# Expert top-k scores copied out of PSUM by ScalarE, and more buffers for the gathered expert rows, in a two-layer diffusion backbone step

## Chip, cores and metric

The kernel runs on one core of a Trainium2 chip. The metric is the device time of one execution in microseconds; a kernel's time is the median of its runs. Engines are named as the profile names them: PE is TensorE (PEld its weight loads), DVE is VectorE, ACT is ScalarE, POOL is GpSimd, SP is SyncE, which here only issues DMAs.

## What is computed

A prompt of 128 tokens and a sample of 512 tokens go through two layers, each a token mixer (attention and gated linear attention, GLA) and a product-key expert mixer (PEER). Prompt and sample meet only in the weights. The change lies in the expert mixer, which is computed for blocks of 128 tokens:

```python
def one_block(xt):                                   # 128 tokens x 1024
    q = (xt @ wq).reshape(128, 8, 2, 128)            # 8 heads, 2 halves
    s = jnp.einsum('thpd,pnd->thpn', q, sub_keys)    # 128 scores for each half
    s1, i1 = lax.top_k(s[:, :, 0], 16)
    s2, i2 = lax.top_k(s[:, :, 1], 16)
    cand = (s1[..., :, None] + s2[..., None, :]).reshape(128, 8, 256)
    sc, ci = lax.top_k(cand, 16)
    idx = ...                                        # 16 experts of 16384, per head
    g = jax.nn.softmax(sc, axis=-1)
    a = jax.nn.gelu(jnp.einsum('td,thkd->thk', xt, u[idx]))
    return jnp.einsum('thk,thkd->td', g * a, v[idx])
```

So each token needs 128 rows of u and 128 rows of v, 4 KB each, chosen by its own top-k.

## The kernel before

**Blocks.** The prompt is one block, the sample four. The prompt's block and two of the sample's (`ROWS`, blocks 0 and 1) fetch the chosen expert rows: one indirect DMA issued by POOL brings, for one of the 128 slots, one row of 4 KB for each of the 128 tokens (512 KB, `gather`, L887). For u, DVE multiplies the fetched tile with the token's activations and sums along the row (`u_rows`, L904); for v, DVE adds the weighted tile to an accumulator (`v_rows`, L934). Below, a **u row** or **v row** is one such slot: a gather of 512 KB and one DVE instruction. The other two sample blocks (`DENSE`, blocks 2 and 3) go the dense way: PE multiplies with all 16384 experts. Their u is streamed in 128 tiles of 512 KB (`uc`, matmuls `hp`), ACT applies the gelu into `Q`, DVE writes for groups of 16 tokens a one-hot selection (`spread`: `A` L1042, `eq` L1047, `bw` L1050), PE turns it into gates (`Gp`, L1057), DVE multiplies `Q` by them (L1062), and PE multiplies with v, streamed in 128 tiles `v` (`vacc`, L1083). The 128 experts of a half key are cut into four chunks of 32 (`CIS`), each with 16 groups of tokens: below, chunk 3 group 2 means the third group of the last chunk. `A`, `eq` and `bw` have two buffers each, so DVE can be two groups ahead of PE.

**Top-k.** `front` makes the indices. For each head PE writes the two sets of 128 scores into a PSUM tile `sc` (L812), and `top16` (L784 to L789) lets DVE search them: MAX8, FIND_INDEX8, MATCH_REPLACE8 read the scores in PSUM, then MAX8 and FIND_INDEX8 read the rest in an SBUF tile `wk`. For the sample, `sc` shares two PSUM buffers (`psm`, tag mm1) with `hp` and `Gp`.

**Buffers.** Gathered tiles live in a ring of `gat` buffers: `PB` = 6 for the prompt, `GB` = 6 for the sample in both layers. The ring also takes the residual rows and three vectors that finish a block (`load_x1`, `load_fin`), which SP loads.

**Order.** Tracks of work are woven by hand-written shares (`weave`), and a scheduler then sorts each engine's instructions by a simulated timeline. Each engine's queue is therefore fixed when the program is built, and the engine takes it in that order. SP issues all direct DMAs in one queue: a load that waits for its buffer holds up the loads behind it.

**Stages**, by the profile: sample mixer of layer 0 beside the prompt's mixer and gathers (to about 1520 us), sample experts of layer 0 beside the prompt's mixer of layer 1 (to 3100), sample mixer of layer 1 beside the prompt's gathers (to 4170), sample experts of layer 1 (to the end). In the experts' stages the gathers go u rows of block 0, v rows of block 0, u rows of block 1, v rows of block 1.

Of the kernel before, what the change touches and what calls it, by code (L numbers as in the profile page):

```python
# [7 lines left out]
F32 = mybir.dt.float32  # L8
# [3 lines left out]
AF = mybir.ActivationFunctionType  # L12
# [13 lines left out]
NK = 128  # L26
# [5 lines left out]
CW = 256  # L32
UC = 256
SB = 4
PB = 6
UBS = (4, 4)
HG = 4
LEAD = (1, 1, 2, 2, 2)
# [11 lines left out]
AB = 12  # L50
QBS = (3, 4)
TG = 16
GB = 6
U0 = 56
YB = 3
PAIRS = [(i, j) for i in range(TOPK) for j in range(TOPK) if (i + 1) * (j + 1) <= TOPK]
# [7 lines left out]
def kernel(ctx: ExitStack, tc, xp, xs, ck, cv, st, cond, adaw, adab, win, wglr,  # L64
                              nrm, w2, gb, gn, wao, wgo, wout, lnp, wq, sk, pu, put, pv, rope, cst, msk,
                              yp, ys, nk_out, nv_out, ns_out):
    nc = tc.nc

    def sided(tr):
        side = ("right", "left")[tr]  # L70
        return lambda name: tc.tile_pool(name=name + str(tr), bufs=1, side=side, reuse_waits="tile")

    def opener(stack, tr):
        mk = sided(tr)
        return lambda name: stack.enter_context(mk(name))
# [15 lines left out]
    def psm(name, tr=0):  # L91
        return ps.tile([128, 512], F32, tag=f"mm{tr}", bufs=2, name=name)
# [690 lines left out]
    def top16(v, i, src, n):  # L783
        nc.vector.max(v[:, 0:8], src)  # L784
        nc.vector.max_index(i[:, 0:8], v[:, 0:8], src)
        wk = sm.tile([128, NK], F32, tag="wk", bufs=2, name="wk")
        nc.vector.match_replace(wk[:, 0:n], v[:, 0:8], src, -3.0e38)  # L787
        nc.vector.max(v[:, 8:16], wk[:, 0:n])
        nc.vector.max_index(i[:, 8:16], v[:, 8:16], wk[:, 0:n])  # L789

    def front(tr, l, b, res, own, groups, near):
# [5 lines left out]
        for n in groups:  # L797
            tv = own.tile([128, HG, 2, TOPK], F32, tag=f"tv{tr}", bufs=2 - tr, name="tv")
            ti = own.tile([128, HG, 2, TOPK], U32, tag=f"ti{tr}", bufs=2 - tr, name="ti")
            for h in range(n):  # L800
                hh = h0 + h
                assert lp[l]["qp", tr] > hh
                if near:
                    qs = [lp[l]["q", tr, 2 * hh + k][:, b * 128:(b + 1) * 128] for k in range(2)]
                else:
                    qT = sm.tile([128, 2, 128], F32, tag="qT", bufs=CB, name="qT")
                    nc.sync.dma_start(qT, tops[tr, l][2 * hh:2 * hh + 2, :, b * 128:(b + 1) * 128]
                                      .rearrange("k p t -> p k t"))
                    qs = [qT[:, k, :] for k in range(2)]
                s = psm("sc", tr)  # L810
                for k in range(2):
                    nc.tensor.matmul(s[:, k * NK:(k + 1) * NK], qs[k], lp[l]["sk"][:, k, :], start=True, stop=True)  # L812
                for k in range(2):
                    top16(tv[:, h, k, :], ti[:, h, k, :], s[:, k * NK:(k + 1) * NK], NK)
                yield 2
# [288 lines left out]
    def weave(*tracks):  # L1104
        live = [[t[0][2], list(t)] for t in tracks]
        while live:
            e = min(live, key=lambda v: v[0])
            g, total, a, b = e[1][0]
            try:
                v = next(g)  # L1110
                e[0] += v * (b - a) / total
                yield v
            except StopIteration:
                e[1].pop(0)
                if e[1]:
                    e[0] = max(e[0], e[1][0][2])
                else:
                    live.remove(e)
# [10 lines left out]
    def take(g, n):  # L1129
        for _ in range(n):  # L1130
            yield next(g)
# [11 lines left out]
    def s_peer(l):  # L1143
        ms, m = parts[l]
        with ExitStack() as st_:
            assert parts["p_peer", l] == "done"
            parts["p_close", l].close()
            p = Peer(1, l, opener(st_, 0)("sgat"), GB)
            r0, r1 = ROWS
            d0, d1 = DENSE  # L1150
            f0, u0 = p.front(r0, LEAD, True), p.u_rows(r0)

            def lead():
                for n in LEAD:
                    yield from take(m, n)
                    yield from take(f0, 3 * n + 1)
                for _ in m:
                    pass

            yield from weave([(lead(), 160.0, 0.0, 1.0)], [(take(u0, U0), 1.5 * U0, UP, 1.0)])  # L1160
            for _ in f0:
                pass
            ms.close()
            parts["s_peer", l] = "open"
            ds = ExitStack()
            p.up = opener(ds, 1)("dense")
            r, f = RF, FF
            yield from weave([(p.dense(p.up, DENSE), 1010.0, DF[0], DF[1])],
                             [(u0, 192.0 - 1.5 * U0, r[0], r[1]), (p.v_rows(r0), 197.0, r[1], r[2]),
                              (p.u_rows(r1), 192.0, r[2], r[3]), (p.v_rows(r1), 197.0, r[3], r[4])],  # L1170
                             [(p.front(d0), 50.0, 0.0, f[0]), (p.front(d1), 50.0, f[0], f[1]),
                              (p.front(r1), 50.0, f[2], f[3])])
        fs = parts["fin"] = ExitStack()
        fp = opener(fs, 0)("fin")
        ds.close()
        yield from p.settle(fp, DENSE)
        if l == L - 1:
            fs.close()
# [22 lines left out]
    def p_front(l):  # L1201
        peers[l] = Peer(0, l, None, PB)
        yield from peers[l].front(0)
# [111 lines left out]
```

## Time and profile before

| | |
|---|---|
| median of 3 runs | 5521.72 us (5514.61 to 5526.49) |
| profiled execution | 5526.76 us |
| its span, first to last instruction | 5525.0 us |
| PE busy | 4570.1 us (83%) |
| DVE busy | 3905.2 us (71%) |
| POOL busy | 2251.5 us (41%) |
| ACT busy | 1041.1 us (19%) |
| mean granted PE clock | 0.894 |

Two engines are busy for most of the time, PE and DVE, and neither all the time: they take turns in being the one that the others wait for. The table of shares hides that; it has to be read stage by stage.

### The profile page before, as it was taken

What the parts mean: (1) busy time and instruction counts of PE and PEld (TensorE: products, weight loads), DVE (VectorE), ACT (ScalarE), POOL (GpSimd) and SP (SyncE); (2) the same over time, 40 slices, a digit from 0 to 9 for tenths busy, and PEclk for the clock granted to TensorE, in tenths of its full rate; (3) what the DMA queues carried; (4) which work ended last, traced back from release to release, by engine and by line L of the source; (5) the groups of instructions that cost most, each with busy time, mean ns of one, the idle gap of its engine ahead of it and who ended that gap; (6) DMA issues with size and microseconds to landing.
All of it is one profiled execution on the core that took longest, in us unless ns stands there. A gap on an engine that the chain in (4) does not pass through costs nothing.

```text
span 5525.0 us, 71758 instructions
## 1 busy us (share of the span) xinstructions
PE 4570.1 (83%) x26668; PEld 3388.7 (61%) x26668; DVE 3905.2 (71%) x8024; ACT 1041.1 (19%) x1860; POOL 2251.5 (41%) x1652
## 2 busy tenths in 40 slices
PE   8879988877776789799999668689877458998998
PEld 5658665655655566467774445578776347675743
DVE  4342368887499996967656798864248999978682
ACT  4231123322211201010000222145221010000000
POOL 0000017675355552343441476620135656245450
PEclk9979998988887799899999778788988679998999
DMA  5325558998388888799996688830447889698995
GB/s 180 117 69 176 190 183 320 318 327 304 135 311 322 326 310 314 249 352 342 369 364 236 215 305 290 300 112 19 133 135 258 323 313 356 214 397 302 409 331 204
DMA packets 472735, 1440.71 MB, mean 261 GB/s; under 512 B 55232, under 2 KB 123968, under 8 KB 472384
## 3 DMA queue, kind: packets, MB, share of 16 engines
q0 software_dynamic: 221184, 805.40, 39.9%
q1 hardware_dynamic: 251200, 630.71, 32.4%
q8 instruction: 209, 3.42, 0.2%
q14 instruction: 142, 1.16, 0.1%
HBM read 1391.29 MB, written 44.63 MB: 260 GB/s over the span
## 4 chain that ended last, share of the span: by engine, by line
DVE 16%; PE 16%; issue 8%; DMA 7%; POOL 2%; ACT 1%; another core or an unknown queue 1%; SPq 0%; DVEq 0%; POOLq 0%; ACTq 0%
DMA gat<-in_pv,idx 4%; PE vacc L1083 4%; DVE gat L904 4%; PE gt L151 3%; DVE acc L934 3%; DMA gat<-in_pu,idx 2%; PE proj L151 2%; PE po L151 2%; POOL gat L887 1%; PE hp L151 1%; DVE A L1042 1%; PE qp L151 1%; DVE Q L1062 1%; DVE bw L1050 1%; PE pTp L626 1%
## 5 line engine op out<-in xcount | busy, mean ns | idle before, releaser
L887 POOL DMA_INDIRECT gat<-in_pu,idx x768 | 991.9, 1292 | 886.8 <-DVE gat L904 382.2
L887 POOL DMA_INDIRECT gat<-in_pv,idx x768 | 962.7, 1253 | 789.4 <-DVE acc L934 468.0
L934 DVE SCALAR_TENSOR_TENSOR acc<-gat,dots,acc 128x1024 f32<-128x1024 f32 x762 | 999.0, 1311 | 155.8 <-DMA gat<-in_pv,idx 141.4
L904 DVE SCALAR_TENSOR_TENSOR gat<-gat,h 128x1024 f32<-128x1024 f32 x768 | 945.1, 1242 | 141.4 <-DMA gat<-in_pu,idx 129.8
L151 PE MATMUL hp<-h2Td,uc 128*128 128x256 f32 x4096 | 947.9, 392 | 76.3 <-DVE wk L787 48.9
L1083 PE MATMUL vacc<-v,Q 128*128 128x512 f32 x2048 | 925.2, 605 | 14.3 <-DMA v<-in_pv 13.6
L151 PEld LDWEIGHTS hp<-h2Td,uc 128*128 128x128 f32 x4096 | 799.3, 197 | 199.7 <-DVE wk L787 52.2
L136 POOL TENSOR_TENSOR wl<-w,wh 128x1024 fp32r<-128x1024 f32 x92 | 232.0, 2521 | 1447.2 <-ACT wh L134 1358.1
L1083 PEld LDWEIGHTS vacc<-v,Q 128*128 128x128 f32 x2048 | 384.7, 193 | 456.5 <-issue 437.0
L134 ACT ACTIVATE wh<-w 128x1024 fp32r<-128x1024 f32 x184 | 194.2, 1057 | 706.4 <-PE proj L151 282.7
L996 ACT ACTIVATE Q<-hp 128x512 f32<-128x512 f32 x128 | 76.4, 597 | 1117.0 <-PE hp L151 1022.7
L151 PE MATMUL proj<-wh,hTh 128*128 128x256 f32 x896 | 264.1, 295 | 7.2 <-DVE sgo L486 3.4
L151 PE MATMUL proj<-wl,hTh 128*128 128x256 f32 x896 | 262.0, 292 | 5.5 <-POOL wl L136 5.5
L151 PE MATMUL proj<-wh,hTl 128*128 128x256 f32 x896 | 263.7, 294 | 0.0
L1057 PEld LDWEIGHTS <-A 128*128 128x128 bf16 x6144 | 174.6, 96 | 132.5 <-issue 61.7
L136 DVE TENSOR_TENSOR wl<-w,wh 128x1024 fp32r<-128x1024 f32 x92 | 127.8, 1389 | 173.6 <-ACT wh L134 163.4
L1057 PE MATMUL Gp<-bw,A 128*128 128x32 bf16 x6144 | 181.0, 177 | 77.4 <-DVE bw L1050 57.3
L151 PE MATMUL po<-V,pT 128*128 128x64 f32 x1600 | 220.0, 279 | 10.2 <-ACT pT L628 8.4
L151 PEld LDWEIGHTS po<-V,pT 128*128 128x128 f32 x1600 | 211.1, 201 | 20.0 <-ACT pT L628 12.7
L151 PE MATMUL modr<-w,csil 128*2 128x256 f32 x768 | 193.9, 405 | 21.4 <-DMA w<-in_adaw 17.7
L618 DVE TENSOR_REDUCE nm<-s 128x1 f32<-128x768 f32 (+1 forms) x160 | 130.9, 819 | 114.0 <-PE s L151 112.7
L151 PEld LDWEIGHTS proj<-wh,hTh 128*128 128x128 f32 x896 | 176.1, 197 | 18.1 <-issue 13.2
(297 smaller groups left out, 7567.1 us busy)
## 6 DMA issues: line engine op xcount, KB each, us to landing
uc<-in_put SPq DMA_DIRECT2D x256, 512.0 KB
v<-in_pv SPq DMA_DIRECT2D x256, 512.0 KB
w<-in_win SPq DMA_DIRECT2D x208, 512.0 KB
w<-in_adaw SPq DMA_DIRECT2D x96, 512.0 KB
w<-in_wq SPq DMA_DIRECT2D x64, 512.0 KB
w<-in_wgo SPq DMA_DIRECT2D x32, 512.0 KB
w<-in_wao SPq DMA_DIRECT2D x32, 512.0 KB
w<-in_wout SPq DMA_DIRECT2D x32, 512.0 KB
```

The source lines that it names most:

```text
L134: nc.scalar.activation(wh, r, AF.Copy)
L136: (nc.vector, nc.gpsimd)[i].tensor_sub(wl, r, f32(wh))
L151: nc.tensor.matmul(out, lt, rt, start=(i == 0), stop=(i == n - 1))
L618: nc.vector.tensor_reduce(nm, s[:, 0:KEYS], axis=AX.X, op=OP.max, negate=True)
L626: nc.tensor.transpose(t[:, (kc - c0) * 128:(kc - c0 + 1) * 128], pr[:, kc * 128:(kc + 1) * 128], ident)
L887: i = nc.gpsimd.indirect_dma_start(out=t, out_offset=None, in_=src, in_offset=bass.IndirectOffsetOnAxis(ap=self.res[b][0][:, k:k + 1], axi ...
L904: nc.vector.scalar_tensor_tensor(u, u, 1.0, h2, op0=OP.mult, op1=OP.mult, accum_out=dots[:, k:k + 1])
L934: nc.vector.scalar_tensor_tensor(acc, v, w_, acc, op0=OP.mult, op1=OP.add)
L996: nc.scalar.activation(q[:, i:i + 2, :].rearrange("p i t -> p (i t)"), t, AF.Gelu_apprx_tanh)
L1042: nc.vector.tensor_tensor(a.rearrange("p t (i w) -> p t i w", w=2), pairs[:, None].to_broadcast([128, TG, NK // 2, 2]), i1[:, sl, None, :] ...
L1057: nc.tensor.matmul(t[:, j * CI:(j + 1) * CI], a[:, j, :], bw[:, j, q, :], start=(q == 0), stop=(q == 2))
L1083: nc.tensor.matmul(accs[i][:, s * 512:(s + 1) * 512], w[:, j, i * 128:(i + 1) * 128], v[:, s * 512:(s + 1) * 512], start=(key == 0), stop= ...
```

## The change

```diff
-PB = 6
+PB = 8
-GB = 6
+GBS = (6, 9)
 ...
                 s = psm("sc", tr)
                 for k in range(2):
                     nc.tensor.matmul(s[:, k * NK:(k + 1) * NK], qs[k], lp[l]["sk"][:, k, :], start=True, stop=True)
+                if tr:
+                    sc = own.tile([128, 2 * NK], F32, tag="scs", bufs=2, name="scs")
+                    nc.scalar.activation(sc, s[:, 0:2 * NK], AF.Copy)
+                    s = sc
                 for k in range(2):
                     top16(tv[:, h, k, :], ti[:, h, k, :], s[:, k * NK:(k + 1) * NK], NK)
 ...
-            p = Peer(1, l, opener(st_, 0)("sgat"), GB)
+            p = Peer(1, l, opener(st_, 0)("sgat"), GBS[l])
```

For the sample (`tr` is 1) an ACTIVATE copies the 128x256 scores of a head into an SBUF tile `scs`, of which there are two, and `top16` reads that; it is 64 copies in all (4 blocks, 8 heads, 2 layers). The prompt's gathers get 8 buffers instead of 6 in both layers, the sample's 9 instead of 6 in layer 1, and 6 as before in layer 0. No other instruction is added or dropped, but the scheduler sorts the queues anew. Lines behind the insertion are four higher in the changed kernel (L934 becomes L938).

DVE, layer 1, sample block 1, from the weighing of its u sums (`dots`) on: `acc` is a v row, `Q`, `A`, `eq` and `bw` belong to the dense blocks' chunk 3. Before:

```order
L917 TENSOR_TENSOR dots<-dots,g 128x128
L918 SCALAR_TENSOR_TENSOR dots<-tt,dots 128x128
L934 SCALAR_TENSOR_TENSOR acc<-gat,dots,acc 128x1024 x64
L1062 TENSOR_TENSOR Q<-Q,Gp 128x16x16
L1042 TENSOR_TENSOR A<-keys,i_32174 128x2048
L1050 TENSOR_TENSOR bw<-eq,gparts 128x1536
L934 SCALAR_TENSOR_TENSOR acc<-gat,dots,acc 128x1024
L1047 TENSOR_TENSOR eq<-keys,i_32175 128x512
```

The same place now:

```order
L921 TENSOR_TENSOR dots<-dots,g 128x128
L1051 TENSOR_TENSOR eq<-keys,i_32287 128x512
L922 SCALAR_TENSOR_TENSOR dots<-tt,dots 128x128
L938 SCALAR_TENSOR_TENSOR acc<-gat,dots,acc 128x1024 x118
L1066 TENSOR_TENSOR Q<-Q,Gp 128x16x16
L1046 TENSOR_TENSOR A<-keys,i_32286 128x2048
L1054 TENSOR_TENSOR bw<-eq,gparts 128x1536
L938 SCALAR_TENSOR_TENSOR acc<-gat,dots,acc 128x1024
L1051 TENSOR_TENSOR eq<-keys,i_32287 128x512
```

The `bw` shown is that of chunk 3 group 2 in both: 64 v rows stood ahead of it, now 118 do. In the same way chunk 2 group 2 stood behind 73 u rows of this block and now stands behind 92. PE's queue in this stage keeps its order but for a few places of 4 to 7 us.

SP, the last loads of the same stage: `v` are the streamed tiles, `gat` the ring, `x1d`, `rowd` and `in_lnp` the residual rows and vectors that finish block 1, `out` its store, `fg`, `fw`, `fb` and `x` the same for blocks 2 and 3. Before:

```order
L1079 DMA v<-in_pv 128x1024 x34
L943 DMA gat<-x1d_22412 128x1024
L1079 DMA v<-in_pv 128x1024 x2
L213 DMA gat<-rowd_9332 128x8x128
L1079 DMA v<-in_pv 128x1024 x2
L219 DMA gat<-in_lnp 128x1024 x2
L1079 DMA v<-in_pv 128x1024 x4
L968 DMA out<-acc 128x1024
L213 DMA fg<-rowd_9332 128x8x128
```

The same place now:

```order
L1083 DMA v<-in_pv 128x1024
L947 DMA gat<-x1d_22476 128x1024
L1083 DMA v<-in_pv 128x1024 x2
L213 DMA gat<-rowd_9332 128x8x128
L219 DMA gat<-in_lnp 128x1024 x2
L1083 DMA v<-in_pv 128x1024 x9
L972 DMA out<-acc 128x1024
L213 DMA fg<-rowd_9332 128x8x128
```

The load `gat<-x1d` now has 65 of the 128 `v` tiles ahead of it where it had 98.

DVE, layer 0, sample mixer, where its gate part begins (`gxl` is the low half of a split that PE multiplies with), beside the prompt's v rows. Before:

```order
L136 TENSOR_TENSOR wl<-w,wh 128x1024
L934 SCALAR_TENSOR_TENSOR acc<-gat,dots,acc 128x1024 x5
L268 TENSOR_TENSOR gxl<-xraw,gxh 128x512 x2
L934 SCALAR_TENSOR_TENSOR acc<-gat,dots,acc 128x1024 x5
L268 TENSOR_TENSOR gxl<-xraw,gxh 128x512
```

The same place now:

```order
L136 TENSOR_TENSOR wl<-w,wh 128x1024
L938 SCALAR_TENSOR_TENSOR acc<-gat,dots,acc 128x1024 x10
L268 TENSOR_TENSOR gxl<-xraw,gxh 128x512
L938 SCALAR_TENSOR_TENSOR acc<-gat,dots,acc 128x1024
L268 TENSOR_TENSOR gxl<-xraw,gxh 128x512
```

The eight `gxl` stood behind 40 to 58 of the prompt's 127 v rows and now stand behind 57 to 82; in layer 1's mixer the sample's instructions likewise stand behind 12 to 20 more of the prompt's rows.

## Rows read from the trace of the kernel before

**Rows 1.** The page: busy time of the engines, and the two DMA queues that matter, q0 with the gathers and q1 with the direct loads (packets, MB, share of the 16 DMA engines).

```profile
PE 4570.1 (83%) x26668; PEld 3388.7 (61%) x26668; DVE 3905.2 (71%) x8024; ACT 1041.1 (19%) x1860; POOL 2251.5 (41%) x1652
...
q0 software_dynamic: 221184, 805.40, 39.9%
q1 hardware_dynamic: 251200, 630.71, 32.4%
```

**Rows 2.** Waits over the whole span (who <- for whom: us in total, times, longest us), those that touch the gathers and the scores.

```profile
DVE acc L934 <- DMA gat<-in_pv,idx: 141.4, 166, 2.8
DVE gat L904 <- DMA gat<-in_pu,idx: 129.8, 126, 5.4
...
PE sc L812 <- DVE wk L787: 59.8, 7, 17.7
...
DVE tv L784 <- PE sc L812: 56.5, 16, 25.2
...
PE hp L151 <- DVE wk L787: 48.9, 11, 10.5
```

**Rows 3.** Groups of instructions over the span (line, engine, operation, tiles, shapes, count | busy us, mean ns | idle before and what ended it): a v row on DVE, a gather's issue on POOL, a 128x256 copy on ACT, and the search for the eight greatest of 128 scores, once with the scores in PSUM (`sc`) and once in SBUF (`wk`).

```profile
L934 DVE SCALAR_TENSOR_TENSOR acc<-gat,dots,acc 128x1024 f32<-128x1024 f32 x762 | 999.0, 1311 | 155.8 <-DMA gat<-in_pv,idx 141.4 <-issue 3.4 <-ACT acc L932 3.3
L887 POOL DMA_INDIRECT gat<-in_pu,idx x768 | 991.9, 1292 | 886.8 <-DVE gat L904 382.2 <-DVE idx L853 181.6 <-issue 113.0
...
L784 DVE MAX8 tv<-sc 128x8 f32<-128x128 f32 x160 | 46.3, 290 | 56.5 <-PE sc L812 56.5
...
L788 DVE MAX8 tv<-wk 128x8 f32<-128x128 f32 x160 | 45.2, 283 | 0.0
...
L544 ACT ACTIVATE kd<-kd 128x256 f32<-128x256 f32 x50 | 19.8, 416 | 136.1 <-DVE kd L543 89.8 <-DVE kd L533 46.1
```

**Rows 4.** Stretches of the last stage from the u rows of block 1 on (from:to, length, busy us and count of PE, PEld, DVE, ACT, POOL, granted PE clock, DMA share, GB/s).

```profile
4825.00:4970.00 145.00, 145.00 (x566) 103.75 (x565) 102.20 (x258) 10.59 (x16) 73.81 (x69) 1.00 1.00 389
4970.00:5080.00 110.00, 88.28 (x906) 50.14 (x902) 96.38 (x153) 0.60 (x1) 60.61 (x42) 0.87 0.84 302
5080.00:5130.00 50.00, 47.99 (x216) 42.05 (x217) 36.19 (x64) 4.86 (x8) 28.90 (x25) 0.95 0.92 348
...
5130.00:5258.00 128.00, 128.00 (x523) 85.61 (x522) 80.90 (x64) 6.04 (x11) 62.42 (x63) 1.00 1.03 409
5258.00:5335.00 77.00, 69.33 (x805) 39.11 (x802) 76.89 (x94) 0.00 (x0) 36.50 (x25) 0.96 0.82 284
```

**Rows 5.** Single lines in parts of that stretch (count: ns min/median/max, first and last start in us): the first 64 u rows of block 1, `bw` of chunk 2 groups 2 to 15, the first 64 v rows of block 1, `bw` of chunk 3 groups 2 to 15, and all `vacc` after the last `Gp`.

```profile
L904 DVE SCALAR_TENSOR_TENSOR gat<-gat,h x64: 1194/1225/1234, 4829.3 to 4969.7; 128x1024 f32<-128x1024 f32 x64
...
L1050 DVE TENSOR_TENSOR bw<-eq,gparts x14: 951/962/977, 4989.6 to 5077.3; 128x1536 bf16<-128x1536 bf16 x14
...
L934 DVE SCALAR_TENSOR_TENSOR acc<-gat,dots,acc x64: 1283/1285/1352, 5129.6 to 5257.7; 128x1024 f32<-128x1024 f32 x64
...
L1050 DVE TENSOR_TENSOR bw<-eq,gparts x14: 948/960/968, 5260.6 to 5332.8; 128x1536 bf16<-128x1536 bf16 x14
...
L1083 PE MATMUL vacc<-v,Q x384: 592/592/1061, 5335.0 to 5506.4; 128*128 128x512 f32 x192
```

**Rows 6.** Waits from 4830 to the end: DVE's for landings, and PE's for its streamed tiles.

```profile
DVE acc L934 <- DMA gat<-in_pv,idx: 67.3, 86, 1.9
...
DVE gat L904 <- DMA gat<-in_pu,idx: 55.7, 58, 4.7
...
PE vacc L1083 <- DMA v<-in_pv: 4.7, 2, 4.3
```

**Rows 7.** The first part of that stage, from the first top-k to chunk 0 group 0: the stretch (columns as in rows 4), and DVE's waits for u rows from 4150 to 4830.

```profile
4171.00:4578.00 407.00, 228.42 (x941) 186.10 (x939) 393.51 (x1192) 46.19 (x66) 248.52 (x190) 0.76 0.88 312
...
DVE gat L904 <- DMA gat<-in_pu,idx: 14.2, 12, 4.7
```

**Rows 8.** Layer 0's sample mixer where its gate part begins: two stretches, 28 of the prompt's v rows and the eight `gxl` (columns as in rows 5), and PE's wait for `gxl` from 1140 to 1350.

```profile
1205.00:1345.00 140.00, 105.73 (x406) 81.45 (x406) 117.94 (x95) 28.70 (x36) 102.52 (x73) 0.85 0.94 346
1345.00:1520.00 175.00, 138.66 (x768) 120.45 (x767) 93.41 (x117) 42.23 (x47) 53.49 (x19) 0.88 0.42 144
...
L934 DVE SCALAR_TENSOR_TENSOR acc<-gat,dots,acc x28: 1277/1285/4004, 1152.6 to 1205.3; 128x1024 f32<-128x1024 f32 x28
...
L268 DVE TENSOR_TENSOR gxl<-xraw,gxh x8: 684/685/693, 1171.2 to 1204.7; 128x512 fp32r<-128x512 f32 x8
...
PE gt L151 <- DVE gxl L268: 18.2, 8, 3.9
```

**Rows 9.** Layer 1's sample mixer beside the prompt's rows: the stretch, and DVE's waits for landings in it.

```profile
3100.00:3640.00 540.00, 385.15 (x2031) 295.35 (x2030) 489.56 (x723) 146.63 (x238) 368.41 (x270) 0.79 0.85 294
...
DVE gat L904 <- DMA gat<-in_pu,idx: 16.0, 17, 2.1
...
DVE acc L934 <- DMA gat<-in_pv,idx: 6.3, 8, 2.2
```

**Rows 10.** Layer 0's sample experts, where the buffers stay six: the stretch before the first `bw`, and PE's waits from 2150 to 2420.

```profile
1500.00:1930.00 430.00, 305.01 (x1345) 246.97 (x1344) 399.32 (x1280) 83.68 (x153) 229.74 (x177) 0.83 0.85 308
...
PE Gp L1057 <- DVE bw L1050: 18.2, 4, 6.7
PE hp L151 <- DVE wk L787: 8.1, 1, 8.1
```

## The prediction, made before the changed kernel had run

> **What bounds the kernel now.** I read four views in this order. The page's shares [rows 1] give PE 83% and DVE 71%, so no engine is full everywhere. The list of waits [rows 2] says what the change could win: DVE waits 271.2 us in all for gathered rows (141.4 for v, 129.8 for u), in many waits of at most 5.4 us; PE waits for the end of a top-k search (`wk`), which frees the PSUM buffers that `sc`, `hp` and `Gp` share, 59.8 us before a new `sc` and 48.9 us before `hp`. The table by stretches then says where such waits count: only where the waiting engine sets the pace. In the first part of the last stage DVE does: busy 393.5 of 407.0 us, PE 228.4 [rows 7], so PE's waits on `wk` there are slack. From 4825 on PE and DVE take turns [rows 4]. While PE streams (145.0 of 145.0 us busy, 128.0 of 128.0), DVE takes gathered rows and the DMA share is 1.00 and 1.03; then DVE makes `bw` for chunk 2's groups, later chunk 3's, PE follows it, and the share falls to 0.84 and 0.82. The single lines [rows 5] give the pace: 64 u rows in 140.4 us, 2.23 us a row, and 64 v rows in 128.1 us, 2.0 a row, though DVE works only 1.23 and 1.29 us on one. So there the rows come at the rate of DMA. 0.524 MB in 2.0 us is 262 GB/s; of the 409 shown that leaves about 147 for PE's tiles. More buffers do not make this faster; they let a few rows more arrive early. The hand-over is tight in the kernel before: PE has streamed until 5258, and the `bw` it needs comes at 5260.6 [rows 4, 5].
>
> **The change part by part.**
>
> *The last sample block of layer 1: +50 us.* What matters is that `bw` of chunk 2 group 2 now stands behind 92 u rows instead of 73, and `bw` of chunk 3 group 2 behind 118 v rows instead of 64.
>
> Step 1. Before, the 73 u rows were done by 4989.6 [rows 5]. PE streams without a gap to 4970 [rows 4]; I put the end of it at 4984 in either kernel. By then some 72 rows will be in (the pace is DMA's; the three additional buffers give three rows). The other 20 come while nothing else streams. No row shows gathers alone; the nearest bounds are 1.28 us (0.524 MB at 409 GB/s [rows 4]), POOL's issue of 1.29, DVE's 1.31 [rows 3], and from above the 2.23 of the row pace. I take 1.4, near the three lower ones, since nothing else streams. 20 x 1.4 = 28: `bw` at 5012, +22.
>
> Step 2. The 14 `bw` to the last took 87.7 us before [rows 5] and DVE's work among them is nearly the same; +22 stays. PE has no gap from there to 5258 (128.0 of 128.0), so it now runs dry at 5280 and needs chunk 3 group 2 by about 5282.
>
> Step 3. The v rows began at 5129.6. The u rows that lay between and behind the `bw` then now lie ahead, so v begins soon after the last `bw` (5077.3 + 22 = 5099), near 5110. Nine rows lie in buffers, the others come at 2.0 us while PE streams: by 5282, 9 + 172/2.0 = 95 rows. The other 23 at 1.4 take 32 us: `bw` at 5314 where it was 5260.6, +54.
>
> Step 4. The 14 groups took 72.2 us; no v row waits among them any more, so 68: −4. Step 5. After them come 384 `vacc` (5335.0 to 5506.4, 171.4 us) at 592 ns, PE alone; the 54 v rows that DVE did meanwhile were hidden there, and this cover is what the change gives up. Sum of the stage's end: +50.
>
> Its bounds. Below: PE's tiles and the rows share one pace throughout. From 4829, 128 u and 118 v rows and some 110 streamed tiles (147 GB/s over the 390 us or so in which PE streams) of 0.524 MB must land before that `bw`; 187 MB at 409 GB/s are 456 us, 5285, or +24 less 4: +20. Above: rows at 2.0 us to the end, 23 x 2.0 = 46, +68, and PE after so long a wait at a lower clock (0.76 is the granted clock where it waits much [rows 7], 0.96 in chunk 3's groups before): +75. SP's queue is a part of the upper bound: the load `gat<-x1d` waits for the buffer of about v row 115, and now the `v` tiles from number 66 on wait behind it instead of from 99 on; PE needs those only after the groups, and there DMA has room, since PE waited 4.7 us for `v` in this stage [rows 6].
>
> [...]
>
> *First half of layer 1's experts (4171 to 4578): −10 us.* DVE sets the pace; its idle time is 13.5 of 407.0, its waits for u rows 14.2 up to 4830 [rows 7]. Nine buffers can win at most that, and 7 us of DVE work stand behind chunk 0 group 0 now instead of ahead. I take −10, between 0 and −20.
>
> *Layer 0's experts, six buffers as before: −10 us.* Here only the copy and the order act. PE waits 18.2 us for `bw` and 8.1 for `wk` [rows 10] in the part where PE sets the pace (that last wait goes with the copy), and `bw` of chunks 2 and 3 stands some 12 us of DVE work earlier. Before that DVE is the busier (399.3 against 305.0 of 430) and gains nothing. I take −10, from −20 to 0.
>
> *Layer 0's mixer: +5 us.* The eight `gxl` stood behind 40 to 58 v rows of the prompt and stand behind 57 to 82. The 28 rows among them took 52.7 us, 1.88 us each with the `gxl`. 25 rows more are 47 us late at that pace, and PE waits for `gxl` already (18.2 us [rows 8]). But PE is busy 105.7 of 140 and 138.7 of 175 us after it, DVE has those rows less to do later, and the DMA share falls to 0.42: most of the delay is caught up. I take +5; −10 if eight buffers remove waits, +30 if PE's idle time (34 and 36 us) is not where it can be used.
>
> *Layer 1's mixer: −5 us.* 12 to 20 more prompt rows stand ahead, up to 20 x 1.24 = 25 us of DVE work, but 22.3 us of waits for landings can go (16.0 + 6.3 [rows 9]) and DVE idles 50 of 540 us. Between −15 and +15.
>
> *The copies: 0.* 64 ACTIVATEs of 128x256. The trace has none from PSUM to SBUF alone of this shape; the nearest, in SBUF, takes 416 ns [rows 3]: 27 us on an engine busy for 19%. Per head it adds one such step and a semaphore between `sc` and the search, and `scs` has two buffers, so it hides behind the search of the head before. Bound: if copies wait in ACT's queue, +10. What they free, the PSUM buffers, counts only as above. The search itself reads SBUF now: MAX8 takes 283 ns there against 290 [rows 3], 7 ns for some 3 operations in 128 searches, 3 us at most.
>
> [...]
>
> **Sum.** 50 − 10 − 10 + 5 − 5 = +30. The profiled execution took 5526.76 us, 5 above the median of the runs: 5557 there, 5552 as a median.
>
> **The rivals.**
>
> *Faster, 5495.* The waits for landings, 271.2 us, 123.0 of them in the last block (67.3 + 55.7 [rows 6]) and 148 elsewhere, are a matter of latency and buffers, not of bandwidth. Then rows land at about 1.4 us: 118 v rows, nine in buffers, are done 109 x 1.4 = 153 us after 5110, and the end of the stage moves by nothing. That pace is the point from which it decides. With the gains above and a fifth of the 148 it is −27. For it: shares of 0.85 to 0.88 elsewhere, and many waits of 2 us. Against: 1.00 and 1.03 in the last block.
>
> *Same, about 5518.* The last block costs its lower bound, +20, since the rows come as early as DMA allows, and the offsets cancel it (20 − 10 − 10 + 5 − 5 = 0, and 3 less for the search). For it: work is only moved, none is added except on ACT. Against: before 4984 and 5258 DMA is already full.
>
> *Much slower, 5595.* The mixers lose what their queues show: +38 of the 47 late in layer 0, and +24, all rows ahead, in layer 1, which makes 50 − 20 + 62 less the overlap of 20. For it: PE waits there for DVE's splits already. Against: there is idle time on both engines to catch up.
>
> **How the numbers follow.** Forecast 5552: 0.62. Faster 0.15, same 0.15, much slower 0.08. The range goes from the faster rival's upper half, 5500, to 5595, the rival above and the upper bounds of the last block together. A measurement of this kernel tells 0.2%, 11 us, from no change: 5511 to 5533. Of the forecast's 0.62, some 0.03 lie within and 0.01 below: faster 0.16, same 0.18, slower 0.66.
>
> **What would show it.** In the profile of the changed kernel: PE waiting 30 to 55 us for `bw` before chunk 3 group 2, near 5280 to 5314, and some 20 before chunk 2's; v rows at 2.0 us while PE streams and near 1.4 after it; no v row between the last groups; a last `vacc` part still of 171 us; fewer waits for `wk`, without the first half of the stage getting shorter by more than 20 us. It is wrong if v rows come faster than 1.5 us while PE streams (then the first rival), or if the last stage begins later than 4171 by over 20 us (then the third).

## The result, and the profile after

The changed kernel is slower. Its median is 5573.78 us (5570.07 to 5577.86, 4 runs) against 5524.1 us of the kernel before on the same chip, a ratio of 1.0092 with a 95% interval of 1.0076 to 1.0108. The profiled execution took 5571.52 us where that of before took 5526.76: +44.8 us, where the prediction had +30. The page hardly shows it: the engines' busy time is that of before [rows 1] to within 3%, so no work was added that matters.

```profile
PE 4566.0 (82%) x26668; PEld 3389.7 (61%) x26668; DVE 3894.2 (70%) x8024; ACT 1068.0 (19%) x1928; POOL 2318.2 (42%) x1652
```

Where the time went is read from the same instruction in both traces. Three marks on PE cut the program: the first `xt` after 2900 (layer 1's mixer begins), the first `h2td` of layer 1 (its experts begin), and the first `Gp` of layer 1 (chunk 0 group 0). The lines give first and last start; the kernel before first, then the changed one.

```profile
L329 PE MATMUL xt<-ident,x x16: 421/421/449, 3068.3 to 3073.7; 128*128 128x128 f32 x16
...
L982 PE MATMUL h2td<-ident,x x16: 421/421/421, 4274.4 to 4277.6; 128*128 128x128 f32 x16
...
L1057 PE MATMUL Gp<-bw,A x3072: 176/176/210, 4578.9 to 5335.0; 128*128 128x32 bf16 x192
```

```profile
L329 PE MATMUL xt<-ident,x x16: 272/363/449, 3042.0 to 3046.0; 128*128 128x128 f32 x16
...
L986 PE MATMUL h2td<-ident,x x16: 421/421/475, 4261.4 to 4264.7; 128*128 128x128 f32 x16
...
L1061 PE MATMUL Gp<-bw,A x3072: 176/176/209, 4560.3 to 5386.3; 128*128 128x32 bf16 x192
```

The changed kernel is 26.3 us ahead at the first mark, 13.0 at the second, 18.6 at the third, and 44.7 behind at the end of the span (5569.7 against 5525.0). So layer 0 gained 26 us, layer 1's mixer lost 13, the first half of its experts gained 6, and the rest of the last stage, from the first `Gp` on, lost 63.

The stretches of that last part (columns as in [rows 4], which they answer to), cut where the changed kernel's work changes:

```profile
4807.00:4984.00 177.00, 160.70 (x666) 112.57 (x665) 124.88 (x295) 12.01 (x20) 110.61 (x88) 0.94 0.98 375
4984.00:5003.00 19.00, 2.11 (x5) 0.57 (x3) 15.41 (x26) 0.00 (x0) 13.23 (x12) 0.67 1.03 410
5003.00:5099.00 96.00, 71.76 (x798) 42.99 (x799) 96.00 (x156) 0.31 (x1) 53.28 (x38) 0.83 0.84 303
5099.00:5279.00 180.00, 171.45 (x691) 121.34 (x689) 125.83 (x99) 10.70 (x17) 126.48 (x98) 0.98 1.02 401
5279.00:5307.00 28.00, 0.14 (x6) 0.04 (x2) 27.28 (x23) 0.00 (x0) 21.43 (x21) 0.59 1.03 409
5307.00:5386.00 79.00, 74.14 (x814) 41.60 (x815) 66.59 (x99) 1.24 (x1) 1.88 (x2) 0.93 0.61 217
```

Two stretches have PE idle up to the next `bw`, 19 and 28 us long, each after a stretch in which it streamed and just before a chunk's groups. DVE works through both (15.4 of 19, 27.3 of 28): it takes gathered rows. The single lines show the pace (as in [rows 5]): the u rows ahead of `bw` of chunk 2 group 2, before (73) and now (92), v rows while PE streams, v rows in the idle stretch (the row that starts at 5277.8 stands in both lines), `bw` of chunk 2 from group 2 on together with the first two of chunk 3, `bw` of chunk 3 from group 2 on, and the `vacc` after the last `Gp`.

```profile
L904 DVE SCALAR_TENSOR_TENSOR gat<-gat,h x73: 1194/1225/1234, 4829.3 to 4986.3; 128x1024 f32<-128x1024 f32 x73
...
L908 DVE SCALAR_TENSOR_TENSOR gat<-gat,h x92: 1192/1225/1227, 4814.4 to 5001.2; 128x1024 f32<-128x1024 f32 x92
...
L938 DVE SCALAR_TENSOR_TENSOR acc<-gat,dots,acc x98: 1283/1284/1289, 5100.3 to 5277.8; 128x1024 f32<-128x1024 f32 x98
...
L938 DVE SCALAR_TENSOR_TENSOR acc<-gat,dots,acc x21: 1284/1285/1286, 5277.8 to 5304.2; 128x1024 f32<-128x1024 f32 x21
...
L1054 DVE TENSOR_TENSOR bw<-eq,gparts x16: 942/950/971, 5004.0 to 5097.0; 128x1536 bf16<-128x1536 bf16 x16
...
L1054 DVE TENSOR_TENSOR bw<-eq,gparts x14: 940/952/965, 5307.1 to 5379.2; 128x1536 bf16<-128x1536 bf16 x14
...
L1087 PE MATMUL vacc<-v,Q x384: 592/592/676, 5386.3 to 5550.7; 128*128 128x512 f32 x192
```

98 rows start within 177.5 us, 1.83 us apart; with PE idle 20 more follow 1.32 us apart. The waits, PE's from the first `Gp` on and then DVE's for rows from 4810 on ([rows 6] of before), name a DMA, DVE and ACT as what PE's idle time waited for (`issue` is idle time for which the trace names nothing):

```profile
PE vacc L1087 <- DMA v<-in_pv: 32.4, 2, 31.6
PE Gp L1061 <- DVE bw L1054: 31.0, 11, 12.0
PE Gp L1061 <- DVE Q L1066: 25.4, 1, 25.4
PE hp L151 <- ACT Q L1000: 13.5, 1, 13.5
PE hp L151 <- issue: 6.6, 10, 1.5
...
DVE acc L938 <- DMA gat<-in_pv,idx: 50.1, 66, 1.3
DVE gat L908 <- DMA gat<-in_pu,idx: 47.6, 46, 4.7
```

The 25.4 us are the wait ahead of chunk 2 group 2. `Q` is the multiply that empties a `Gp` buffer; the one that ended this wait was begun at 5010.9, behind the 92 rows, `bw` (5004.0) and five more u rows. The 31.6 us are the wait ahead of chunk 3 group 2, and there the trace names not `bw` but a `v` tile. PE's timeline (start, us, instruction, idle before and what ended it) shows both waits, and how near `bw` and the `v` tile were:

```profile
5011.55 1.44 PE L1061 MATMUL Gp<-bw,A 128*128 128x32 bf16 x48 [25.43 <-DVE Q L1066]
...
5278.61 0.53 PE L1061 MATMUL Gp<-bw,A 128*128 128x32 bf16 x15
5310.79 5.65 PE L1087 MATMUL vacc<-v,Q 128*128 128x512 f32 x8 [31.65 <-DMA v<-in_pv]
5316.28 0.98 PE L1061 MATMUL Gp<-bw,A 128*128 128x32 bf16 x33
```

`bw` was begun at 5307.1, the `v` tile landed by 5310.8. That tile stands in SP's queue behind `gat<-x1d`, which waits for a ring buffer, hence for a v row: SP stood 35.1 us before it, issued it at 5301.6, and the next `v` load at 5302.0. Experiments had to tell these two apart.

### The profile page after: what moved, and what is told of

Read it like the earlier page. It is cut to its first block, busy times and chain, and to the rows that moved or that the text cites. A ratio compares the mean times of both kernels' runs of the same rounds, so it can differ in the third digit from the quotient of the medians.

```text
span 5569.7 us, 71795 instructions
## 1 busy us (share of the span) xinstructions
PE 4566.0 (82%) x26668; PEld 3389.7 (61%) x26668; DVE 3894.2 (70%) x8024; ACT 1068.0 (19%) x1928; POOL 2318.2 (42%) x1652
## 4 chain that ended last, share of the span: by engine, by line
PE 41%; DVE 26%; issue 15%; DMA 12%; POOL 3%; ACT 2%; another core or an unknown queue 0%; SPq 0%; POOLq 0%; DVEq 0%; ACTq 0%
PE vacc L1087 9%; PE proj L151 7%; DVE gat L908 7%; PE gt L151 7%; DMA gat<-in_pu,idx 5%; PE hp L151 4%; DVE acc L938 3%; DMA gat<-in_pv,idx 3%; POOL gat L891 3%; PE po L151 3%; PE modr L151 2%; PE qp L151 2%; PE s L151 1%; PE kv L466 1%; DVE A L1046 1%
## 5 line engine op out<-in xcount | busy, mean ns | idle before, releaser
L891 POOL DMA_INDIRECT gat<-in_pu,idx x768 | 1033.5, 1346 | 796.8 <-DVE idx L857 205.5
L891 POOL DMA_INDIRECT gat<-in_pv,idx x768 | 989.4, 1288 | 650.4 <-DVE acc L938 305.5
L938 DVE SCALAR_TENSOR_TENSOR acc<-gat,dots,acc 128x1024 f32<-128x1024 f32 x762 | 994.9, 1306 | 115.6 <-DMA gat<-in_pv,idx 98.8
L1000 ACT ACTIVATE Q<-hp 128x512 f32<-128x512 f32 x128 | 76.3, 597 | 795.8 <-PE hp L151 739.9
```

The source lines that it names most:

```text
L891: i = nc.gpsimd.indirect_dma_start(out=t, out_offset=None, in_=src, in_offset=bass.IndirectOffsetOnAxis(ap=self.res[b][0][:, k:k + 1], axi ...
L938: nc.vector.scalar_tensor_tensor(acc, v, w_, acc, op0=OP.mult, op1=OP.add)
L1000: nc.scalar.activation(q[:, i:i + 2, :].rearrange("p i t -> p (i t)"), t, AF.Gelu_apprx_tanh)
```

## Experiments

Theory A: the larger ring of layer 1 costs the time through the order. The scheduler puts more rows ahead of `bw` on DVE, and PE, which has run out of streamed work, waits for DVE. Rivals: B, the additional gathers in flight take DMA from PE's tiles; C, the copies cost it; D, SP's queue (`v` behind `gat<-x1d`).

The kernel before ran at a median of 5504 to 5514 us on the chips of the three sets, and 5524 on that of the result. So ratios are compared, and of the traces only lengths: "last part" is the time from the first `Gp` of layer 1 to the end of the span. Each comes from one trace. Kernels with the same buffers in layer 1 and the same order agree to 3 us on different chips (1009.4, 1010.7 and 1010.1; 935.1 and 935.0; 914.6 and 911.9), but before and e_pb, with equal rows ahead, lie 12 us apart, which no run explains. "Rows ahead" are the v rows of block 1 that the program puts ahead of `bw` of chunk 3 group 2.

| kernel | copy | prompt, layer 0, layer 1 buffers | rows ahead | ratio to before (95% interval) | first `Gp`, span: last part (us) |
|---|---|---|---|---|---|
| before | no | 6, 6, 6 | 64 | 1 | 4578.9, 5525.0: 946.1 |
| changed | yes | 8, 6, 9 | 118 | 1.0092 (1.0076 to 1.0108) | 4560.3, 5569.7: 1009.4 |
| e_hold | yes | 8, 6, 9, order of before | 64 | 1.0003 (0.9990 to 1.0015) | 4557.7, 5507.9: 950.2 |
| e_copy | yes | 6, 6, 6 | 62 | 0.9911 (0.9893 to 0.9930) | 4518.6, 5453.7: 935.1 |
| e_gb | no | 6, 6, 9 | 119 | 1.0141 (1.0115 to 1.0167) | 4564.7, 5573.0: 1008.3 |
| e_pb | no | 8, 6, 6 | 64 | 1.0012 (0.9999 to 1.0025) | 4574.5, 5508.3: 933.8 |
| e_copy_67 | yes | 6, 6, 7 | 82 | 0.9953 (0.9940 to 0.9967) | 4524.3, 5487.6: 963.3 |
| e_copy_65 | yes | 6, 6, 5 | 43 | 0.9874 (0.9859 to 0.9889) | 4524.4, 5439.0: 914.6 |
| e_copy_64 | yes | 6, 6, 4 | 28 | 0.9997 (0.9984 to 1.0010) | 4525.8, 5497.4: 971.6 |
| e_hold6 | yes | 6, 6, 9, order of before | 64 | 0.9928 (0.9914 to 0.9941) | 4518.5, 5469.0: 950.5 |
| e_x1act | yes | 8, 6, 9 | 118 | 1.0111 (1.0095 to 1.0126) | 4568.7, 5579.4: 1010.7 |
| e_x1pool | yes | 8, 6, 9 | 118 | 1.0101 (1.0084 to 1.0117) | 4545.5, 5555.6: 1010.1 |
| e_copy_p5_55 | yes | 5, 5, 5 | 43 | 0.9943 (0.9925 to 0.9960) | 4559.3, 5471.2: 911.9 |
| e_copy_pb | yes | 8, 6, 6 | 62 | 0.9969 (0.9956 to 0.9981) | 4555.6, 5490.6: 935.0 |

**The order alone (e_hold).** All buffers and copies stay; the place of block 1's rows in DVE's queue is made that of before. `BEHIND` lists for each chunk how many rows stand ahead of each group's `bw`, and `tc.issue_after` puts a row behind that `bw` in DVE's queue.

```diff
+BEHIND = {2: (0, 0, 73, 74, 78, 80, 83, 84, 88, 89, 92, 93, 98, 98, 104, 104),
+          3: (0, 0, 65, 70, 72, 73, 75, 76, 78, 79, 81, 82, 83, 85, 86, 88)}
 ...
+    def behind(tr, l, b, c, k):
+        if not tr or l != L - 1 or b != ROWS[1]:
+            return nullcontext()
+        g = max(j for j in range(16) if BEHIND[c][j] <= k)
+        return tc.issue_after(marks[c, g]) if g > 1 else nullcontext()
 ...
-                    nc.vector.scalar_tensor_tensor(acc, v, w_, acc, op0=OP.mult, op1=OP.add)
+                    with behind(tr, self.l, b, 3, k):
+                        nc.vector.scalar_tensor_tensor(acc, v, w_, acc, op0=OP.mult, op1=OP.add)
```

> The changed kernel with everything kept (copy, 8 and 9 buffers), but in layer 1 each row of sample block 1 is queued on DVE behind the bw behind which it stood in the kernel before (73 u rows and 64 v rows ahead of group 2 of chunks 2 and 3, instead of 92 and 118). Theory A (the queue order on DVE costs the time: bw stands behind 54 more v rows): the last block loses its +60 us, and the kernel comes out at 5500 to 5515 us, 10 to 25 us under the kernel before, with the second v-tile wait of 31 us gone. Theory B (the additional gathers in flight cost the time by taking DMA from PE's streamed tiles): the order does not matter, 5560 to 5580. Theory C (the copies cost it): 5560 to 5580 as well.

1.0003, and the last part falls from 1009.4 to 950.2 us with nine buffers in the ring. The order takes back 59 us between the two traces and 49 by the ratios, which refutes B and C as causes of these. It does not yet separate A from D: with the rows the scheduler also moved the load `gat<-x1d` back in SP's queue, behind 94 of the 128 `v` tiles (98 before, 65 in the changed kernel). The expected gain of 10 to 25 us over before did not come: the last part is still 16 us longer than e_pb's with six buffers on the same chip (933.8; the 946.1 of before are from another chip). PE's waits in it (as above, who <- for whom) name three things that are short or absent in e_copy, the `v` tiles (5.1 us there), the gelus `ACT Q` (1.2) and a wait of `hp` for which the trace names no engine:

```profile
PE Gp L1074 <- DVE bw L1066: 30.6, 8, 12.0
PE vacc L1100 <- DMA v<-in_pv: 15.4, 3, 12.1
PE hp L153 <- ACT Q L1012: 12.8, 1, 12.8
PE hp L153 <- issue: 10.2, 1, 10.2
```

The waits for `v` tiles come after the last `Gp`, while SP waits 14.4 us for a ring buffer for `gat<-x1d`; from the last `Gp` to the end e_hold takes 201.3 us and e_pb 190.3. So most of the 16 us lies there, and SP's queue may have a share in them; no run tested that.

**The copy alone (e_copy).**

```diff
-PB = 8
+PB = 6
-GBS = (6, 9)
+GBS = (6, 6)
```

> The copy alone, 6 buffers everywhere as before. Theory A: the last stage keeps the order of before (70 u rows and 62 v rows ahead of group 2), and the gain of layer 0's experts (26 us in the trace of the changed kernel) stays: 5495 to 5510. Theory B says the same. Theory C (the copies cost the time): 5550 to 5575.

0.9911: the copy by itself makes the kernel some 48 us faster (5458.2 against 5505.7 us), more than expected. C is refuted; what the change lost, it lost with the buffers. The groups of the search and of PE's `sc` and `hp` in this kernel, against [rows 2] and [rows 3]:

```profile
L784 DVE MAX8 tv<-scs 128x8 f32<-128x128 f32 x128 | 30.1, 275 | 16.7 <-ACT scs L815 16.7
L815 ACT ACTIVATE scs<-sc 128x256 f32<-128x256 f32 x64 | 24.4, 381 | 258.2 <-PE sc L812 168.1 <-DVE wk L787 46.9 <-DVE g L865 13.2
...
PE hp L151 <- ACT scs L815: 46.8, 7, 16.8
```

PE's 59.8 us of waits of `sc` for `wk` are gone, though its waits of `sc` for the DMA that brings `qT` rose from 50.9 to 82.8; those of `hp` became waits for the copy (46.8 in all), and 43.9 of them lie between 4171 and 4600, in the first half of layer 1's experts, where DVE sets the pace (busy 399.5 of the 407.0 us from 4171 to 4578, PE 238.7). Against e_pb and e_gb, which have no copy and ran on the same chip, layer 1's mixer begins at 3024.4 instead of 3050.1 and 3053.9: 26 to 30 us are gained in layer 0. Against e_gb another 10 are gained in layer 1's mixer and 7 in the first half of its experts, and the last part is no shorter than e_pb's.

**The two buffer numbers alone (e_gb, e_pb).**

```diff
 # e_gb, against the kernel before
-GB = 6
+GBS = (6, 9)
 ...
-            p = Peer(1, l, opener(st_, 0)("sgat"), GB)
+            p = Peer(1, l, opener(st_, 0)("sgat"), GBS[l])
 # e_pb, against the kernel before
-PB = 6
+PB = 8
 ...
-GB = 6
+GBS = (6, 6)
```

> The 9 buffers of the sample in layer 1 alone, no copy, prompt at 6. Theory A: 104 u... that is 99 u rows and 119 v rows stand ahead of group 2 of chunks 2 and 3, so the last block loses 60 to 70 us and nothing offsets it elsewhere: 5575 to 5595. Theory B: also slower, 5570 to 5595. Theory C: as before, 5515 to 5530.

> The 8 buffers of the prompt alone, no copy, sample at 6. The order of the last stage is that of the kernel before. Theory A: only the mixers' orders move, 5515 to 5535. If the prompt's buffers cause the 24 us that the changed kernel loses in layer 1's mixer: 5535 to 5550. Theories B and C: 5520 to 5530.

e_gb 1.0141: nine buffers without anything to offset them cost 73 us, and the last part is as long as the changed kernel's (1008.3). e_pb 1.0012: no change that can be told.

**A step at a time (e_copy_67, e_copy_65, e_copy_64).** As e_copy, with `GBS` (6, 7), (6, 5), (6, 4).

> The copy, prompt at 6, sample at 6 and 7 buffers: the scheduler puts 78 u rows and 82 v rows ahead of group 2 of chunks 2 and 3 (70 and 62 with the copy and 6 buffers, 92 and 118 in the changed kernel). Theory A (each further row ahead delays bw, by about 1.4 us once PE has run dry): 20 v rows more cost some 20 to 28 us against the copy alone, ratio to the kernel before 0.995 to 0.997. Rival B2 (9 buffers cost by something that begins only when the ring is large, for instance SP's load of the residual rows): as the copy alone, 0.991.

> The copy, prompt at 6, sample at 6 and 5 buffers: 60 u rows and 43 v rows ahead of group 2. Theory A: the hand-over was tight at 62 v rows, so earlier bw gain at most 5 us before PE's own work bounds the stage; fewer buffers make DVE wait more where it sets the pace: ratio 0.990 to 0.995. If DVE's rows in the first half of the layer are what six buffers pay for: 0.995 or more.

> The copy, prompt at 6, sample at 6 and 4 buffers: 52 u rows and 28 v rows ahead of group 2 (60 and 43 with 5, 70 and 62 with 6, 78 and 82 with 7). If each step of the ring keeps giving some 20 us, ratio 0.983; if bw is no longer late there and DVE's waits for landings take over, 0.988 to 0.995, and the first half of the stage is longer.

The last part grows with the rows ahead: 43 rows 914.6 us, 62 rows 935.1, 82 rows 963.3, 118 rows 1009.4, or 1.1, 1.4 and 1.3 us for a row more, about what a row costs when nothing else streams (1.32 us in the changed kernel). Two other places move with the ring: the u rows ahead of chunk 2 group 2 (60, 70, 78, 92) and the `v` tiles ahead of `gat<-x1d` on SP (116, 99, 86, 65). e_copy_67 came out as expected. Five buffers were expected to gain 5 us at most from an earlier `bw` and gained 20: `bw` of chunk 3 group 2 came 7 us earlier after the first `Gp` (661.6 against 668.8), the time from there to the last `Gp` fell by 6, and that from the last `Gp` to the end by 7.5. Four buffers are too few, and cost more than either expectation had (0.983, or 0.988 to 0.995). `bw` of chunk 3 group 2 comes 685.0 us after the first `Gp`, 23 later than with five buffers though fewer rows are ahead of it: up to the last `Gp` DVE's waits for rows to land are 140 us where they are 97 with five. And PE is done with `vacc` at 5448 while DVE still takes v rows; the tail of PE, the stretch after it, and DVE's waits from 5283 on:

```profile
5283.00:5448.00 165.00, 164.91 (x385) 72.72 (x384) 96.58 (x78) 0.00 (x0) 73.30 (x75) 1.00 0.99 377
5448.00:5497.00 49.00, 0.00 (x0) 0.00 (x0) 28.27 (x67) 3.61 (x3) 1.43 (x2) 0.55 0.46 154
...
DVE acc L938 <- DMA gat<-in_pv,idx: 72.6, 72, 3.5
```

With 28 rows ahead, 99 come after that `bw`, 78 of them after the last `Gp`; the last of them starts at 5456.3, and the end of block 1 and the loads that finish blocks 2 and 3 come behind it, so the span ends 49 us after PE's work where it ends 20 us after it in e_copy. So there is a best point between: rows ahead of `bw` make PE wait, rows behind it must fit under the last `vacc`, and the ring must be large enough for the rows to keep coming.

**Nine buffers in the order of six (e_hold6).** e_hold with `PB` = 6.

> The copy, prompt at 6, sample at 6 and 9 buffers, with the rows of block 1 of layer 1 queued behind the same bw as in the kernel before: nine buffers with the order of six. Theory A: the last block keeps the time of the copy alone, since DMA sets the pace of the rows while PE streams: ratio 0.989 to 0.993. If more buffers hide landings (the rival of the prediction): 0.985 or less. If they cost by themselves: 0.995 or more.

0.9928, within what was expected, 0.0017 above e_copy: even in an order that does not harm, nine buffers give nothing over six. The last part is 950.5 us, as in e_hold, and 15 longer than e_copy's, which was expected to be kept. So of what nine buffers cost (the last part of e_gb is 74 us longer than e_pb's), the order explains the greater part, and some 15 us stay open. The rival of the prediction that expected landings to be hidden is refuted.

**SP's queue (e_x1act, e_x1pool).** The changed kernel, with the residual rows of layer 1's gathered blocks loaded through another queue, so that no `v` tile stands behind them.

```diff
-            nc.sync.dma_start(x, x1_dram[self.tr, self.l][b * 128:(b + 1) * 128, :])
+            eng = nc.scalar if self.tr == 1 and self.l == 1 and b in ROWS else nc.sync
+            eng.dma_start(x, x1_dram[self.tr, self.l][b * 128:(b + 1) * 128, :])
```

(e_x1pool has `nc.gpsimd` for `nc.scalar`.)

> The changed kernel with the residual rows of the two gathered sample blocks of layer 1 loaded by ACT's queue instead of SP's, so that no v tile waits behind them. In the changed kernel PE waited 31.7 us for a v tile that came at 5310.8, and bw came at 5307. Theory A: the v tile was only late beside bw; PE then waits for bw instead, and the time is 0 to 5 us shorter than the changed kernel's: ratio 1.007 to 1.011. Rival: SP's queue is what the last block lost: 0.998 to 1.003.

> The changed kernel with the residual rows of the two gathered sample blocks of layer 1 loaded through POOL's queue, where only the gathers behind them in the same ring wait, so that neither SP's v tiles nor ACT's gelus stand behind them (with ACT's queue the wait moved to ACT). Theory A (the order on DVE): bw of chunk 3 group 2 still comes at about 5305, and PE waits for it in place of the v tile: ratio to the kernel before 1.006 to 1.010. Rival (SP's queue is what the last block lost): 0.996 to 1.003.

1.0111 and 1.0101, just above what was expected and no faster than the changed kernel: with `v` free of `gat<-x1d` and DVE's order kept, the whole loss stays, so D is refuted as its cause, and with e_hold this leaves the order on DVE. e_x1act itself tells little: on ACT the same load held up the gelu behind it for 58.7 us, and PE idled 49.6 us. In e_x1pool nobody stands behind the load, and PE's timeline at the same place shows what was under the wait for the `v` tile:

```profile
5252.13 3.68 PE L1088 MATMUL vacc<-v,Q 128*128 128x512 f32 x8
5301.59 1.44 PE L1062 MATMUL Gp<-bw,A 128*128 128x32 bf16 x48 [45.78 <-DVE Q L1067]
5308.45 1.46 PE L1062 MATMUL Gp<-bw,A 128*128 128x32 bf16 x48 [5.42 <-DVE bw L1055]
```

PE waits for `Q` and `bw`, both behind the rows on DVE, and no shorter. The 31.6 us for the `v` tile had been a second wait that ended at nearly the same time.

**The prompt's buffers and fewer of all (e_copy_pb, e_copy_p5_55).** As e_copy, with `PB` = 8, and with `PB` = 5 and `GBS` (5, 5).

> The copy and 8 buffers for the prompt, sample at 6. In the traces the 8 buffers cost some 20 us in layer 1's mixer, and with them the copy's gain in layer 0 is 28 us where it is 45 without. If that is right, 30 to 40 us are lost against the copy alone: ratio 0.996 to 0.999. If the changes add up as single runs (0.9911 and 1.0012): 0.991 to 0.993.

> The copy, prompt at 5, sample at 5 and 5 buffers. Against the copy with 6, 6 and 5 (0.9874) the prompt's rows stand less far ahead of the sample's instructions in both mixers, and the rows of layer 0 less far ahead of bw. Theory A says a gain of 5 to 15 us, 0.984 to 0.987; if six buffers hide landings there, 0.990 or more.

e_copy_pb 0.9969: with the copy, eight buffers for the prompt cost 0.6%, some 32 us, though without it they cost nothing. So the parts do not add up. From the first `xt` to the first `h2td` e_copy needs 1193.9 us (3024.4 to 4218.3), e_copy_pb 1219.1 (3038.5 to 4257.6), e_gb, without copy, 1203.5 (3053.9 to 4257.4), and e_pb 1221.7 (3050.1 to 4271.8): the eight buffers make layer 1's mixer 18 to 25 us longer. All six kernels with eight need 1215.7 to 1221.7, all seven with six 1193.9 to 1206.1. With the copy they also make layer 0's gain smaller, as the first `xt` at 3038.5 shows against 3021.3 in e_copy_64, which has six and ran on the same chip. e_copy_p5_55 0.9943 missed the expected gain: five buffers everywhere are worse than five in layer 1 alone, and its first `Gp` comes at 4559.3 where that of e_copy_64, with six in the other places and on the same chip, comes at 4525.8. In layer 1's last block the ring was too deep, in the other places five are too few. Taken one after the other, the three parts of the change are −0.9% for the copy (e_copy), +0.6% for the prompt's buffers (e_copy_pb) and +1.2% for the sample's (the changed kernel).

The fastest kernel is e_copy_65, 0.9874 (0.9859 to 0.9889): the copy, and a smaller ring in layer 1 instead of a larger one.

## Why the prediction was right, and where not

The direction, its mechanism and its place were right; the terms were mis-sized by 4 to 21 us each.

**The last block, +50 forecast, +63 measured.** Counted from the first `Gp`, since the changed kernel came to it 18.6 us earlier, the delays were: first `bw` behind the u rows +33 (forecast +22), last `bw` of chunk 2 +31 (+22), PE dry +39 (+22), `bw` of chunk 3 group 2 +65 (+54), last `Gp` +70 (+50), end +63 (+50). *Step 1* was too small by 11 us. Its price for a row was nearly right: from the first u row to that `bw` it took 160.3 us with 73 rows (4829.3 to 4989.6) and 189.6 with 92 (4814.4 to 5004.0), 1.5 us for each of the 19 rows more. But the step took off some 6 us for rows that would be in by 4984, and the u rows began 4 us later after the first `Gp` than before. PE also lost 13.5 us to a wait that the prediction did not have, `hp` for a gelu (`ACT Q`). ACT's timeline shows it. The gelus stand behind an exponential of the top-k of block 1, which waits 40.5 us for DVE's search:

```profile
4879.32 1.28 ACT L860 ACT_TABLE_LOAD   x1
4921.15 0.26 ACT L860 ACTIVATE g<-g 128x64 f32<-128x64 f32 x1 [40.54 <-DVE si L789]
4921.42 1.28 ACT L1000 ACT_TABLE_LOAD   x1
4922.72 1.09 ACT L1000 ACTIVATE Q<-hp 128x512 f32<-128x512 f32 x2
```

e_hold has the same wait (12.8 us) and e_copy not (1.2), so it does not come from the rows ahead of `bw`. But it did not cost the 13 us. Up to that `bw` DVE waited for rows to land (47.6 us from 4814 to 5004) and never for PE, and PE then idled 25.4 us for DVE, so the wait lay in time that PE had to spare; and e_x1act, with the buffers of the changed kernel, has 0.7 us of it, and its `bw` of chunk 3 group 2 came no earlier (749.6 us after the first `Gp`, 746.8 in the changed kernel).

*Step 2* kept the delay as it was, and 8 us were added: from the last `bw` of chunk 2 (5089.9) PE ran dry 189 us later, at 5279.1, where before it took 181 (5077.3 to 5258.5). PE idled about that much (7.9 of 24 us) before `hp` from 5123 to 5147; the trace puts 1.6 us of it down to streamed tiles and names no engine for 6.6. *Step 3* was nearly right: 2.0 us a row while PE streams measured 1.83, 1.4 without measured 1.32, and PE idled 28 us before `bw` where the working had 32 to 34. *Step 4* forecast a gain of 4 us and got none (72.1 us from 5307.1 to 5379.2): nine v rows still lay among the groups, where the step had none (23 before), and the last `Gp` came 79 us after the `bw` of group 2 where it had come after 74. *Step 5* held in kind, and the tail was 7 us shorter, 164.4 us (171.4 before); why is not shown. What the prediction said of SP's queue, that PE needs the `v` tiles behind `gat<-x1d` only after the groups, was wrong, since the groups of chunk 3 take `v` tiles too; e_x1pool shows that it cost nothing because `bw` came no earlier.

**The copies, 0, and layer 0, −10 and +5.** Layer 0 gained 26 us where −5 was forecast, and the copy alone is worth 48. The mechanism was named (PE's waits for `wk`, and `bw` of chunks 2 and 3 earlier on DVE), but its price was bounded at 20 by the waits listed in one stretch [rows 10]. The term failed because those waits were taken as the whole gain; what else the copy moves, the top-k of the later blocks and all that needs their indices, had no price in it. That this is the rest of the gain is argued, no run splits it; the traces show the place. From layer 0's first `Gp` to its last it took 1016.2 us before and 985.9 in the changed kernel (1011.6 in e_gb, 972.9 in e_copy), and half of these 30 us is PE's idle time, 76.3 before and 60.6 now. The +5 of layer 0's mixer was wrong too: its experts' first `h2td` came 7 us earlier (1616.1, before 1623.5). The two terms that the prediction derived from rows alone came out as 381 ns for a copy (416 was used) and 275 ns for MAX8 from SBUF, 15 less than the 290 from PSUM in the kernel before [rows 3] (7 was used).

**Layer 1's mixer, −5 forecast, +13 measured.** The step that failed took the removed waits for landings as a gain and the rows ahead as caught up; it is the third rival's term (+24, all rows ahead) that came nearer. Of the 22.3 us of waits for landings that were to go, 7 went (from 3100 to 3640, v rows from 6.3 to 0.2, u rows only from 16.0 to 15.1); e_pb against e_gb and e_copy_pb against e_copy put 18 to 25 us on the prompt's eight buffers. That it is the order, as in the last block, is argued from the 12 to 20 rows ahead; no run put the rows back there.

**The first half of layer 1's experts**, −10 forecast, measured −6 (18.6 less 13.0). The forecast put it down to the nine buffers, but from the first `h2td` to the first `Gp` e_gb, with nine and no copy, needs 307.3 us, before 304.5, and e_copy, with six and the copy, 300.3: the 6 us came with the copy.

**The rivals.** The rivals "faster" and "same" fell with the pace that the first of them named as deciding it: 1.83 us a row, not under 1.5. That the upper rival's mixer and the last block's upper bound both came true in part, while layer 0 gave more back, is why +45 lies so near to +30; the errors, +13, −21, +18 and +4, partly cancelled, which is luck. One side sum of the prediction does not come out: the terms that the faster rival names add up to about −50, not −27. The forecast does not hang on it.

## What to carry to other kernels

A deeper ring of buffers is not free when a scheduler sorts the queues by when its model thinks data is there: here it put 54 more rows ahead of the instruction on DVE for which PE was about to wait. Before adding buffers, look at which instruction the bounding engine will want next and count what the new order puts ahead of it; multiply by the pace of those rows with DMA full, and by their pace alone (here 1.83 and 1.32 us). And measure the parts of a change one by one: here one part was worth 48 us, another cost 73, and the opposite of the second gained again.

## What the runs showed of the hardware that was not expected

DMA moved 401 GB/s over 180 us with gathers and streamed tiles mixed (48.56 and 23.59 MB), and in the 28 us in which PE was idle the share was 1.03 and the rate 409 GB/s (11.02 MB of gathers, 0.43 of direct loads), as in [rows 4] while PE streamed. A gathered row came 1.32 us after the one before when the queue of streamed tiles stood still (no `v` load was issued from 5264.1 to 5302.0), and 1.83 us while it ran. At 1.32 DVE was full too (27.3 of 28 us busy, 1.28 on a row), so whether gathers alone could come faster is not shown. A wait that the trace names alone can hide a second one that ends within 4 us of it: the `v` tile at 5310.8 covered `bw` at 5307.1, and taking the first away (e_x1pool) gained nothing.
